# Sixty 16 KB runs of one head of tile 41 stored apart, computed in eight groups ahead of tiles 40 to 47

## The chip, the cores and the metric

The kernel runs on one core of a Trainium2 chip. The metric is the device time of one execution in microseconds (us). The kernel before takes 300.39 us, the median of three runs (300.27 to 300.64). A profiled execution is a separate one: 300.63 us, of which the trace covers a span of 298.8 us from the first to the last instruction.

## The reference

```python
batch, n_heads, seq_t, seq_s, channels = 8, 12, 512, 512, 64
x: (8, 12, 512, 64) float32;  y: (8, 12, 512, 64) float32

def reference(x, y):
    return np.einsum('bhtc,bhsc->bhts', x, y).astype(np.float32)
```

There are 96 heads. For each, a 512 x 64 matrix is multiplied by the transpose of another, and a 512 x 512 float32 result of 1 MB is written. Inputs are 2 x 12.6 MB, the output is 100.7 MB, so four fifths of all traffic are stores.

## The kernel before

**Tiles.** An output tile holds two heads, u = 0 and u = 1, four heads apart in memory. There are 48 of them (o = 0 to 47), four to each of 12 groups. A tile is a slot of SBUF of 128 partitions x 4096 float32, 2 MB. Partition 2q + u holds eight neighbouring output rows of head u, rows 8q to 8q + 7, one after the other: 16 KB that are also contiguous in DRAM. Such 16 KB are called a run here: a tile has 64 runs of each head. There are five slots; loads of x and y (2 MB each, 12 in all) use them too.

**Preparing a group.** ACT, DVE and POOL cast loaded x and y to bf16 into a buffer `keep` (`compress`, the copies at L139 and L141). DVE and POOL spread x so that the two heads of a tile stand in different rows of the contraction with zeros between (`mix`, L141). DVE transposes x and y by 32 x 32 blocks (`transposes`, L206 and L215) into xT and yT, of which there are two each, for even and odd groups. `prepare(i)` emits the transposes of group i and the mixing for group i + 1. From about 62 us on all inputs are loaded, and `keep` falls empty bit by bit.

**A tile.** Eight matmuls of 128 x 128 by 128 x 512 make it, four into each half of PSUM, pm0 and pm1 (`four`, L229 to L237). ACT copies each half into the slot (`result`, L330, the ACTIVATE at L337; 128 x 2048 float32). Then SP issues the 2 MB store (`store`, L323, L328). PE's stream is a loop, `all_products` (L240): six turns of eight tiles, with waits on two semaphores, `ev` for ACT's evictions and `tr` for the transposes.

**Order.** Each engine runs its instructions in the order in which the Python code emits them; `emit` and `need` add the semaphore waits. A slot is free for the tile five later once its store has landed. A DMA is issued by SP in order too: an SP instruction that waits holds up the stores behind it. A store of 128 partitions is spread over 16 DMA engines, eight runs each; each engine works through its own queue in order.

**The corner.** `SPLIT` is tile 41. Of head u = 0 of this tile only a quarter of each run, 4 KB (`N` = 2 x 512 elements, the first two of eight rows), is stored from the slot, by an extra SP store behind that of head u = 1. The other six rows of each run (12 KB, `LEFT` = 6) are computed a second time by `corner` (L257): DVE picks the columns of xT that belong to chosen runs into `picked` (L275), so that the runs land on chosen partitions; PE multiplies them in eight groups of up to four matmuls (96 or 16 rows of PSUM, L295), inside the loop's sixth turn under an `If`; DVE and ACT take turns to copy the groups into the emptied part of `keep` (L141 and L139); and three DMAs store them: by SP 20 runs that lie on 4 partitions ("corner", L314), by POOL 12 runs on 3 partitions and 32 runs on 8 partitions ("side"). `FEW` lists these sets: partitions (in fours) from, to, and runs on each.

In the order of instructions the corner stands between tile 41 and tile 42. On PE the list `held` of its matmuls and waits is put into the loop at that place, and ends with a wait for the last copies of both PSUM halves (L307). On ACT and DVE the copies stand behind the evictions of tile 41, and SP waits for all copies before its corner DMA, which stands ahead of the store of tile 42.

The last lines of the order before:

```python
        for o in range(V, V * NH):
            result(o, slot())
            if o == SPLIT:
                corner()
            if o % V == V - 1:
                prepare(o // V + 2)
        all_products()
        need("pool", [("dmaside", ticks["dmaside"])])
        need("dve", [("dmacorner", ticks["dmacorner"])])
```

V is 4, NH is 12.

Of the kernel before, what the change touches and what calls it, by code (L numbers as in the profile page):

```python
# [9 lines left out]
def kernel(  # L10
# [22 lines left out]
    nc = tc.nc  # L33
# [9 lines left out]
    K = 8  # L43
    E = R // K
    D = 32
    SLOTS = 5
    TURNS = NH // 2
    SPLIT = V * NH - 2 * V + 1
    LEFT = 6
    N = (K - LEFT) * S  # L50
    GROUP = 4
    FEW = ((0, 4, 5), (5, 8, 4), (16, 24, 4))
    fp32 = mybir.dt.float32
    bf16 = mybir.dt.bfloat16
    u32 = mybir.dt.uint32
# [27 lines left out]
    engines = {"act": nc.scalar, "dve": nc.vector, "pool": nc.gpsimd, "pe": nc.tensor, "sp": nc.sync}  # L83
    sems, ticks, known, snaps, writer, readers = {}, {}, {e: {} for e in engines}, {}, {}, {}

    def need(name, points, known_by=None, held=None):

        best = {}
        for p, v in points:
            if known[name].get(p, 0) < v:  # L90
                best[p] = max(best.get(p, 0), v)
        for p, v in list(best.items()):
            if any(snaps[q, w].get(p, 0) >= v for q, w in best.items() if q != p):
                del best[p]
        if known_by is not None:
            assert all(p in dict(known_by) and v <= dict(known_by)[p] for p, v in best.items())
        for p, v in best.items():
            if held is not None:
                held.append((p, v))
            elif known_by is None:  # L100
                engines[name].wait_ge(sems[p], v)  # L101
            known[name][p] = v
            for q, w in snaps[p, v].items():
                known[name][q] = max(known[name].get(q, 0), w)

    lanes = {"act": ("act", "ev"), "dve": ("dve", "tr")}

    def emit(name, make, reads=(), writes=(), dma=None, lane=None, known_by=None, held=None):

        points = [writer[r] for r in (*reads, *writes) if r in writer]  # L110
        points += [v for w in writes for v in readers.get(w, ())]
        if name == "pool" and name in ticks:
            points.append((name, ticks[name]))
        need(name, points, known_by, held)
        p, step = (lane or name, 1) if dma is None else (f"dma{dma}", 16)
        if p not in sems:
            sems[p] = tc.alloc_semaphore(p)
        if held is not None:
            held.append(make)
        elif make is not None:  # L120
            make().then_inc(sems[p], step)
        at = (p, ticks.get(p, 0) + step)
        ticks[p] = at[1]
        snaps[at] = {**known[name], p: at[1]}
        if dma is None:
            for q in lanes.get(name, (name,)):
                snaps[at][q] = ticks.get(q, 0)
        for r in reads:
            readers.setdefault(r, []).append(at)
        for w in writes:  # L130
            writer[w], readers[w] = at, []

    made_slots, loaded, held = [], {}, []
    in_front = ["dve", "pool", "dve", "act"]

    def copy(name, dst, src, reads, writes):
# [12 lines left out]
    def slot():  # L149
        made_slots.append(len(made_slots) % SLOTS)  # L150
        return made_slots[-1]
# [71 lines left out]

    def products(o, k):
        half, pm = o // V % 2, k // 4
        emit("pe", None, [("xT", half), ("yT", half)], [("pm", pm)],
             known_by=[("ev", 2 * o + pm + 1), ("tr", o // V + 1)])

    def four(j, pm):  # L229
        half, h = divmod(j, V)  # L230
# [9 lines left out]
    def all_products():  # L240

        with nc.tensor.Fori(0, TURNS, 1) as t:
            for j in range(2 * V):
                if j % V == 0:
                    nc.tensor.wait_ge(sems["tr"], t * 2 + j // V + 1)
                for pm in range(2):
                    nc.tensor.wait_ge(sems["ev"], t * (4 * V) + 2 * j + pm + 1)
                    four(j, pm).then_inc(sems["pe"], 1)
                if j == SPLIT % (2 * V):
                    with nc.tensor.If(t == SPLIT // (2 * V)):  # L250
                        for step in held:
                            if callable(step):
                                step().then_inc(sems["pe"], 1)
                            else:
                                nc.tensor.wait_ge(sems[step[0]], step[1])

    def corner():  # L257

        half, h = divmod(SPLIT % (2 * V), V)
        xT = xTs[half].bitcast(bf16).rearrange("p (k h q u) -> p k h q u", k=K, h=V, u=2)  # L260
        yT = yTs[half].bitcast(bf16)
        most = max(many for _, _, many in FEW)
        kept = keep[:, :most * LEFT * S].bitcast(fp32)
        runs = kept.rearrange("p (j n) -> p j n", j=most)
        dst = ov[SPLIT // V, h][:, 0, N:]
        picked = keep[:, 3 * NG * R // 2 * D:].bitcast(bf16)[:, :most * LEFT * 96].rearrange(
            "p (j k m) -> p j k m", j=most, k=LEFT
        )
        under = [("yb", 1, b, ch) for b in range(NG - 3, NG - 1) for ch in range(2)]
        first = 0  # L270
        for lo, hi, many in FEW:
            rows = (hi - lo) * many
            emit(
                "dve",
                lambda: nc.vector.tensor_copy(  # L275
                    picked[:, :many, :, 4 * lo:4 * hi:4],
                    xT[:, K - LEFT:, h, first:first + rows, 0].rearrange("p k (e j) -> p j k e", j=many),
                ),
                [("xT", half)],
                [("picked", lo)] + (under if lo == 0 else []),  # L280
            )
            first += rows
        places = [[("xk", i)] for i in range(NG - 1)]
        for i in range(0, NG - 1, 2):
            places.append([("yb", 0, b, ch) for b in (i, i + 1) if b < NG - 1 for ch in range(2)])
        banks = [divmod(b, LEFT) for b in range(most * LEFT)]
        for g in range(0, len(banks), GROUP):
            part = banks[g:g + GROUP]
            pm = g // GROUP % 2
            m = 96 if part[0][0] < most - 1 else 16  # L290

            def make(part=part, pm=pm, m=m):

                for b, (j, k) in enumerate(part):
                    last = nc.tensor.matmul(  # L295
                        pms[pm][:m, b, :], picked[:, j, k, :m], yT[:, h * S:(h + 1) * S],
                        start=True, stop=True,
                    )
                return last

            emit("pe", make, [("picked", lo) for lo, _, _ in FEW] + [("yT", half)], [("pm", pm)], held=held)
            copy(
                "act" if pm else "dve", kept[:m, g * S:(g + len(part)) * S],
                pms[pm].rearrange("p j s -> p (j s)")[:m, :len(part) * S],
                [("pm", pm)], places[g // GROUP],
            )
        need("pe", [v for pm in range(2) for v in readers[("pm", pm)]], held=held)  # L307
        first = 0
        for lo, hi, many in FEW:
            rows = (hi - lo) * many  # L310
            name = "pool" if lo else "sp"
            emit(
                name,
                lambda: engines[name].dma_start(  # L314
                    dst[first:first + rows].rearrange("(e j) n -> e j n", j=many),
                    runs[4 * lo:4 * hi - 3:4, :many],
                ),
                reads=[w for place in places for w in place],
                dma="side" if lo else "corner",
            )  # L320
            first += rows

    def store(o, s):  # L323
        i, h = divmod(o, V)
        to, src = ov[i, h], slots[s]
        parts = [(to, src)] if o != SPLIT else [(to[:, 1], src[1::2]), (to[:, 0, :N], src[0::2, :N])]
        for to, src in parts:
            emit("sp", lambda: nc.sync.dma_start(to, src), reads=both(s), dma=s)  # L328

    def result(o, s):  # L330

        for k in range(0, K, 4):
            pm = k // 4
            products(o, k)
            emit(
                "act",
                lambda: nc.scalar.activation(  # L337
                    slots[s][:, k * S:(k + 4) * S], pms[pm].rearrange("p j s -> p (j s)"), COPY
                ),
                [("pm", pm)],  # L340
                [("slot", s, pm)],
                lane="ev",
            )
        store(o, s)
# [9 lines left out]
    with tc.tile_critical():  # L354
# [36 lines left out]
                transposes(1)  # L391
        prepare(2)
        for o in range(V, V * NH):
            result(o, slot())
            if o == SPLIT:
                corner()
            if o % V == V - 1:
                prepare(o // V + 2)
        all_products()
        need("pool", [("dmaside", ticks["dmaside"])])  # L400
        need("dve", [("dmacorner", ticks["dmacorner"])])
        for i, name in enumerate(("dve", "dve", "dve", "dve", "act")):
# [31 lines left out]
```

## Time and profile before

| | us |
|---|---|
| median of three runs | 300.39 (300.27 to 300.64) |
| the profiled execution | 300.63 |
| its span | 298.8 |
| outside the span | 1.8 |
| ACT busy | 217.9 (73%) |
| DVE busy | 161.6 (54%) |
| PE busy | 144.7 (48%) |
| POOL busy | 57.9 (19%) |
| moved by DMA | 125.87 MB, 421 GB/s over the span |

How to read the profile. The page gives the span in 40 equal slices of 7.47 us, with each engine's busy share in tenths, the clock granted to TensorE (PEclk), the share of time in which the 16 DMA engines were busy, and the rate in GB/s. The groups of instructions give for each line, engine and shape the count, the busy time and the mean of one in ns, and then how long the engine was idle ahead of them and what ended that. The timeline lists instructions in order of time, neighbours of one kind merged: start, time, engine, line and tile, count, and the idle time ahead with what ended it. The stage table gives busy time of each engine in chosen stretches of the span, with the clock, the DMA share and the rate. The trace also holds every DMA packet with its start, its time, its size and its queue, and the moment at which each of the 16 DMA engines reports its part of a transfer.

### The profile page before, as it was taken

What the parts mean: (1) busy time and instruction counts of PE and PEld (TensorE: products, weight loads), DVE (VectorE), ACT (ScalarE), POOL (GpSimd) and SP (SyncE); (2) the same over time, 40 slices, a digit from 0 to 9 for tenths busy, and PEclk for the clock granted to TensorE, in tenths of its full rate; (3) what the DMA queues carried; (4) which work ended last, traced back from release to release, by engine and by line L of the source; (5) the groups of instructions that cost most, each with busy time, mean ns of one, the idle gap of its engine ahead of it and who ended that gap; (6) DMA issues with size and microseconds to landing.
All of it is one profiled execution on the core that took longest, in us unless ns stands there. A gap on an engine that the chain in (4) does not pass through costs nothing.

```text
span 298.8 us, 1363 instructions
## 1 busy us (share of the span) xinstructions
PE 144.7 (48%) x408; PEld 39.3 (13%) x414; DVE 161.6 (54%) x80; ACT 217.9 (73%) x113; POOL 57.9 (19%) x26
## 2 busy tenths in 40 slices
PE   0000040547665663867475665676475667475400
PEld 0000010111111110211111111111111112121100
DVE  2167897999929594915809439076292535600000
ACT  1665676999999996786868686767777775589900
POOL 3399999991000000000000000000000000010000
PEclk9999995657789997565956767756857767979965
DMA  7999999999999999999999999999999999999997
GB/s 265 430 428 432 430 430 428 428 432 432 425 432 430 434 428 429 434 430 428 430 432 429 432 436 428 430 436 423 425 432 434 430 421 428 421 388 430 421 421 316
DMA packets 8875, 125.87 MB, mean 421 GB/s; under 512 B 1128, under 2 KB 1128, under 8 KB 1192
## 3 DMA queue, kind: packets, MB, share of 16 engines
q1 hardware_dynamic: 8680, 125.29, 98.6%
q0 software_dynamic: 192, 0.54, 0.5%
q8 instruction: 1, 0.02, 0.0%
q14 instruction: 2, 0.02, 0.0%
HBM read 25.17 MB, written 100.66 MB: 421 GB/s over the span
## 4 chain that ended last, share of the span: by engine, by line
DMA 54%; ACT 27%; issue 5%; PE 4%; DVE 3%; another core or an unknown queue 1%; SPq 0%; ACTq 0%
DMA out_dram<-slot 41%; ACT slot L337 25%; DMA slot<-in_y_dram 7%; DMA slot<-in_x_dram 6%; DVE keep L141 3%; ACT keep L139 2%; PE pm L295 2%; PE pm L234 2%; SPq L157 0%; ACTq L101 0%; SPq L429 0%; SPq L354 0%
## 5 line engine op out<-in xcount | busy, mean ns | idle before, releaser
L337 ACT ACTIVATE slot<-pm 128x2048 f32<-128x2048 f32 x96 | 173.7, 1894 | 38.2 <-DMA out_dram<-slot 35.0
L234 PE MATMUL pm<-yT,xT 128*128 128x512 bf16 x378 | 135.6, 502 | 132.0 <-ACT slot L337 92.4
L206 DVE STREAM_TRANSPOSE xT<-xb 128x2048 uint32<-128x2048 uint32 x12 | 46.8, 3897 | 69.4 <-PE pm L234 67.0
L234 PEld LDWEIGHTS pm<-yT,xT 128*128 128x128 bf16 x384 | 35.9, 114 | 230.7 <-ACT slot L337 152.0
L139 ACT ACTIVATE keep<-slot 128x4096 bf16<-128x4096 f32 (+1 forms) x12 | 36.5, 3044 | 21.5 <-DMA slot<-in_x_dram 16.3
L141 DVE COPY xb<-keep 32x2048 bf16<-32x2048 bf16 x36 | 47.0, 1305 | 1.0
L141 DVE CAST keep<-slot 64x2048 bf16<-64x2048 f32 x12 | 36.1, 3010 | 17.1 <-DMA slot<-in_y_dram 16.9
L314 POOL DMA_DIRECT2D out_dram<-keep x2 | 1.1, 558 | 192.6 <-DVE keep L141 192.6
L141 POOL COPY xb<-keep 32x2048 bf16<-32x2048 bf16 x12 | 36.2, 3017 | 9.2 <-ACT keep L139 8.4
L215 DVE STREAM_TRANSPOSE yT<-keep 128x1024 uint32<-128x1024 uint32 x12 | 23.1, 1928 | 0.0
L141 POOL CAST keep<-slot 64x2048 bf16<-64x2048 f32 x6 | 17.8, 2973 | 1.4 <-DMA slot<-in_y_dram 0.8
L141 DVE COPY keep<-pm 96x2048 f32<-96x2048 f32 (+1 forms) x4 | 9.1, 2285 | 10.5 <-PE pm L295 10.5
L295 PE MATMUL pm<-yT,keep 128*96 128x512 bf16 (+1 forms) x30 | 9.2, 446 | 4.9 <-DVE keep L141 2.8
L139 ACT ACTIVATE keep<-pm 96x2048 f32<-96x2048 f32 (+1 forms) x4 | 6.6, 1657 | 5.4 <-PE pm L295 5.4
L295 PEld LDWEIGHTS pm<-yT,keep 128*96 128x96 bf16 (+1 forms) x30 | 3.4, 130 | 11.0 <-DVE keep L141 4.5
L371 DVE MEMSET xb<- 128x2048 uint32 x1 | 1.8, 1765 | 1.4 <-SPq L354 1.4
L139 ACT ACT_TABLE_LOAD x1 | 1.3, 1283 | 1.0 <-SPq L354 1.0
L371 POOL MEMSET xb<- 128x2048 uint32 x1 | 1.8, 1823 | 0.0
L362 POOL DMA_DIRECT2D spare<-in_x_dram x1 | 0.7, 701 | 1.2 <-SPq L354 1.2
L275 DVE COPY keep<-xT 128x120 bf16<-128x120 bf16 (+2 forms) x3 | 0.7, 355 | 0.0
L418 POOL MEMSET const-float32-0.0<- 128x1 f32 x1 | 0.1, 98 | 0.2 <-issue 0.2
L418 POOL MEMSET const-float32-1.0<- 128x1 f32 x1 | 0.1, 98 | 0.0
(2 smaller groups left out, 0.2 us busy)
## 6 DMA issues: line engine op xcount, KB each, us to landing
out_dram<-slot SPq DMA_DIRECT2D x47, 2048.0 KB, 20.5
slot<-in_x_dram SPq DMA_DIRECT2D x6, 2048.0 KB, 17.7
slot<-in_y_dram SPq DMA_DIRECT2D x6, 2048.0 KB, 20.8
out_dram<-slot SPq DMA_DIRECT2D x1, 1024.0 KB, 16.9
out_dram<-keep POOLq DMA_DIRECT2D x1, 384.0 KB, 6.1
out_dram<-slot SPq DMA_DIRECT2D x1, 256.0 KB, 18.6
out_dram<-keep SPq DMA_DIRECT2D x1, 240.0 KB
out_dram<-keep POOLq DMA_DIRECT2D x1, 144.0 KB, 5.6
```

Source lines behind the costliest of these rows:

```text
L139: lambda: nc.scalar.activation(dst, src, COPY)
L141: else engines[name].tensor_copy(dst, src),
L206: lambda: nc.vector.transpose(xTs[half].rearrange("p (k r e) -> p k e r", k=K, e=E), xbs[half].rearrange("p (k e c) -> p k e c", k=K, e=E),),
L215: lambda: nc.vector.transpose(yTs[half].rearrange("p (r j) -> p j r", r=D), ybs[half][b].rearrange("p (j c) -> p j c", c=D),),
L234: last = nc.tensor.matmul(pms[pm][:, b, :], xT[:, 4 * pm + b, h, :], yT[:, h * S:(h + 1) * S], start=True, stop=True,)
L275: lambda: nc.vector.tensor_copy(picked[:, :many, :, 4 * lo:4 * hi:4], xT[:, K - LEFT:, h, first:first + rows, 0].rearrange("p k (e j) -> p ...
L295: last = nc.tensor.matmul(pms[pm][:m, b, :], picked[:, j, k, :m], yT[:, h * S:(h + 1) * S], start=True, stop=True,)
L314: lambda: engines[name].dma_start(dst[first:first + rows].rearrange("(e j) n -> e j n", j=many), runs[4 * lo:4 * hi - 3:4, :many],),
L337: lambda: nc.scalar.activation(slots[s][:, k * S:(k + 4) * S], pms[pm].rearrange("p j s -> p (j s)"), COPY),
L362: lambda: nc.gpsimd.dma_start(spare[0:17:4, :, :D // 2], xv[0, 0:5].rearrange("p (a b c) -> p a b c", a=2, c=D)[:, :, 0, :D // 2]),
L371: lambda: engines[name].memset(xbs[half], 0.0),
L418: nc = _bacc.Bacc("TRN2", target_bir_lowering=False, num_devices=1)
```

## The change

The work of the corner is taken apart into three functions and spread.

- The runs stored apart are now 60 whole runs (16 KB, all eight rows) of head u = 0, four runs on each of 15 partitions (`MANY` = 4), instead of 64 runs of 12 KB. The remaining four runs of that head are stored from the slot, by a store of their own of four partitions (`APART` = 60). Bytes in all are the same.
- `pick` (DVE, three copies) is emitted after tile 36.
- `piece(g, pm)` is one group of four matmuls with 96 rows and its copy by DVE, and is emitted one ahead of each tile from 40 to 47, eight groups in all. A group uses one half of PSUM; the tile behind it begins with the other half: for even tiles the order of halves is pm1, pm0. So the halves strictly take turns on PE. ACT no longer copies any of these groups.
- `send` issues the three DMAs after the eighth group, ahead of the evictions and the store of tile 47: SP 16 runs on 4 partitions, POOL 12 runs on 3 and 32 runs on 8.
- PE's loop has five turns (40 tiles, `LOOPED`) and no `If`; tiles 40 to 47 and the groups follow it as straight code.

```diff
-    TURNS = NH // 2
-    SPLIT = V * NH - 2 * V + 1
-    LEFT = 6
-    N = (K - LEFT) * S
+    TURNS = NH // 2 - 1
+    LOOPED = 2 * V * TURNS
+    SPLIT = LOOPED + 1
+    MANY = 4
     GROUP = 4
-    FEW = ((0, 4, 5), (5, 8, 4), (16, 24, 4))
+    GROUPS = MANY * K // GROUP
+    FEW = ((0, 4), (5, 8), (16, 24))
+    APART = MANY * sum(hi - lo for lo, hi in FEW)
...
     def products(o, k):
         half, pm = o // V % 2, k // 4
-        emit("pe", None, [("xT", half), ("yT", half)], [("pm", pm)],
-             known_by=[("ev", 2 * o + pm + 1), ("tr", o // V + 1)])
+        reads, writes = [("xT", half), ("yT", half)], [("pm", pm)]
+        if o < LOOPED:
+            emit("pe", None, reads, writes, known_by=[("ev", 2 * o + pm + 1), ("tr", o // V + 1)])
+        else:
+            emit("pe", lambda: four(o % (2 * V), pm), reads, writes)
...
-                if j == SPLIT % (2 * V):
-                    with nc.tensor.If(t == SPLIT // (2 * V)):
-                        for step in held:
-                            if callable(step):
-                                step().then_inc(sems["pe"], 1)
-                            else:
-                                nc.tensor.wait_ge(sems[step[0]], step[1])
-
-    def corner():
+
+    def pick():
...
-                    picked[:, :many, :, 4 * lo:4 * hi:4],
-                    xT[:, K - LEFT:, h, first:first + rows, 0].rearrange("p k (e j) -> p j k e", j=many),
+                    picked[:, :, :, 4 * lo:4 * hi:4],
+                    xT[:, :, h, first:first + rows, 0].rearrange("p k (j e) -> p j k e", j=MANY),
...
+    def piece(g, pm):
+
+        half, h = divmod(SPLIT % (2 * V), V)
+        yT = yTs[half].bitcast(bf16)
+
+        def make():
+
+            for b in range(GROUP):
+                j, k = divmod(g * GROUP + b, K)
+                last = nc.tensor.matmul(
+                    pms[pm][:96, b, :], picked[:, j, k, :], yT[:, h * S:(h + 1) * S],
+                    start=True, stop=True,
+                )
+            return last
+
+        emit("pe", make, [("picked", lo) for lo, _ in FEW] + [("yT", half)], [("pm", pm)])
+        copy(
+            "dve", kept[:96, g * GROUP * S:(g + 1) * GROUP * S],
+            pms[pm].rearrange("p j s -> p (j s)")[:96],
+            [("pm", pm)], places[g],
+        )
+
+    def send():
+
+        dst = ov[SPLIT // V, SPLIT % V][:, 0]
         first = 0
-        for lo, hi, many in FEW:
-            rows = (hi - lo) * many
+        for lo, hi in FEW:
+            rows = (hi - lo) * MANY
             name = "pool" if lo else "sp"
             emit(
                 name,
                 lambda: engines[name].dma_start(
-                    dst[first:first + rows].rearrange("(e j) n -> e j n", j=many),
-                    runs[4 * lo:4 * hi - 3:4, :many],
+                    dst[first:first + rows].rearrange("(j e) n -> e j n", j=MANY),
+                    runs[4 * lo:4 * hi - 3:4],
                 ),
...
-        parts = [(to, src)] if o != SPLIT else [(to[:, 1], src[1::2]), (to[:, 0, :N], src[0::2, :N])]
+        parts = [(to, src)] if o != SPLIT else [(to[:, 1], src[1::2]), (to[APART:, 0], src[2 * APART::2])]
...
     def result(o, s):
 
-        for k in range(0, K, 4):
+        for k in (4, 0) if o >= LOOPED and o % 2 == 0 else (0, 4):
             pm = k // 4
...
         for o in range(V, V * NH):
+            if o == LOOPED:
+                all_products()
+            if o >= LOOPED:
+                piece(o - LOOPED, o % 2)
+            if o == V * NH - 1:
+                send()
             result(o, slot())
-            if o == SPLIT:
-                corner()
             if o % V == V - 1:
                 prepare(o // V + 2)
-        all_products()
+            if o == LOOPED - V:
+                pick()
         need("pool", [("dmaside", ticks["dmaside"])])
```

More of the change, by code (lines that the diff above doesn't have):

```diff
@@ L84, with need @@
     sems, ticks, known, snaps, writer, readers = {}, {}, {e: {} for e in engines}, {}, {}, {}
-    def need(name, points, known_by=None, held=None):
+    def need(name, points, known_by=None):
         best = {}
@@ L97, in need @@
         for p, v in best.items():
-            if held is not None:
-                held.append((p, v))
-            elif known_by is None:
+            if known_by is None:
                 engines[name].wait_ge(sems[p], v)
@@ L106, with emit @@
     lanes = {"act": ("act", "ev"), "dve": ("dve", "tr")}
-    def emit(name, make, reads=(), writes=(), dma=None, lane=None, known_by=None, held=None):
+    def emit(name, make, reads=(), writes=(), dma=None, lane=None, known_by=None):
         points = [writer[r] for r in (*reads, *writes) if r in writer]
@@ L113, in emit @@
             points.append((name, ticks[name]))
-        need(name, points, known_by, held)
+        need(name, points, known_by)
         p, step = (lane or name, 1) if dma is None else (f"dma{dma}", 16)
@@ L117, in emit @@
             sems[p] = tc.alloc_semaphore(p)
-        if held is not None:
-            held.append(make)
-        elif make is not None:
+        if make is not None:
             make().then_inc(sems[p], step)
@@ L131, in emit @@
             writer[w], readers[w] = at, []
-    made_slots, loaded, held = [], {}, []
+    made_slots, loaded = [], {}
     in_front = ["dve", "pool", "dve", "act"]
@@ L248, in all_products @@
                     four(j, pm).then_inc(sems["pe"], 1)
-                if j == SPLIT % (2 * V):
-                    with nc.tensor.If(t == SPLIT // (2 * V)):
-                        for step in held:
-                            if callable(step):
-                                step().then_inc(sems["pe"], 1)
-                            else:
-                                nc.tensor.wait_ge(sems[step[0]], step[1])
-    def corner():
+    kept = keep[:, :MANY * K * S].bitcast(fp32)
+    runs = kept.rearrange("p (j n) -> p j n", j=MANY)
+    picked = keep[:, 3 * NG * R // 2 * D:].bitcast(bf16)[:, :MANY * K * 96].rearrange(
+        "p (j k m) -> p j k m", j=MANY, k=K
+    )
+    places = [[("xk", i)] for i in range(NG - 1)]
+    for i in range(0, NG - 1, 2):
+        places.append([("yb", 0, b, ch) for b in (i, i + 1) if b < NG - 1 for ch in range(2)])
+    places[-1] += [("yb", 1, 0, ch) for ch in range(2)]
+    def pick():
         half, h = divmod(SPLIT % (2 * V), V)
         xT = xTs[half].bitcast(bf16).rearrange("p (k h q u) -> p k h q u", k=K, h=V, u=2)
[L261 to L268, printed above, removed]
         under = [("yb", 1, b, ch) for b in range(NG - 3, NG - 1) for ch in range(2)]
         first = 0
-        for lo, hi, many in FEW:
-            rows = (hi - lo) * many
+        for lo, hi in FEW:
+            rows = (hi - lo) * MANY
             emit(
@@ L282, in corner @@
             first += rows
[L283 to L307, printed above, removed]
+    def piece(g, pm):
[14 more added lines that the diff above has]
+            [("pm", pm)], places[g],
+        )
+    def send():
+        dst = ov[SPLIT // V, SPLIT % V][:, 0]
         first = 0
-        for lo, hi, many in FEW:
-            rows = (hi - lo) * many
+        for lo, hi in FEW:
+            rows = (hi - lo) * MANY
             name = "pool" if lo else "sp"
```

## The prediction, made before the changed kernel ran

> **What bounds the kernel now.** I read first the slices of the page, for the resource that is never idle.
>
> ```profile
> PEclk9999995657789997565956767756857767979965
> DMA  7999999999999999999999999999999999999997
> GB/s 265 430 428 432 430 430 428 428 432 432 425 432 430 434 428 429 434 430 428 430 432 429 432 436 428 430 436 423 425 432 434 430 421 428 421 388 430 421 421 316
> ```
>
> DMA is full between the ends, at about 430 GB/s, with one dip: slice 35, 261 to 269 us, 388 GB/s. Second, the stage table around that dip.
>
> ```profile
> 261.00:266.00 5.00, 4.12 (x11) 1.29 (x12) 0.04 (x1) 3.29 (x2) 1.11 (x2) 0.66 0.97 401
> 266.00:268.00 2.00, 1.11 (x5) 0.31 (x4) 0.00 (x0) 2.00 (x3) 0.00 (x0) 1.00 0.67 275
> 268.00:297.00 29.00, 8.29 (x32) 2.47 (x32) 0.00 (x0) 16.06 (x10) 0.00 (x0) 0.81 1.00 425
> ```
>
> From 266 to 268 us the engines are busy for 67%. Counted in the packets, all 16 have work without a gap from 5 us to 266.5 us and again from 267.7 us to the end of the data at 297.28 us; the hole costs 0.80 us per engine in the mean. Third, the timeline, for who makes the hole.
>
> ```profile
> 247.59 2.29 DVE L141 COPY keep<-pm 96x2048 f32<-96x2048 f32 x1 [6.16 <-PE pm L295]
> 248.16 1.91 SPq L328 DMA_DIRECT2D out_dram<-slot  x2
> 249.99 1.87 ACT L139 ACTIVATE keep<-pm 96x2048 f32<-96x2048 f32 x1 [1.85 <-PE pm L295]
> ...
> 261.07 0.82 SPq L314 DMA_DIRECT2D out_dram<-keep  x1
> 261.35 1.11 POOL L314 DMA_DIRECT2D out_dram<-keep  x2 [192.64 <-DVE keep L141]
> ...
> 262.71 21.35 ACT L337 ACTIVATE slot<-pm 128x2048 f32<-128x2048 f32 x12 [2.51 <-remote]
> ...
> 266.38 18.24 SPq L328 DMA_DIRECT2D out_dram<-slot  x6
> ```
>
> Tile 41's stores go out at 248.16, the next full store at 266.38: ACT evicts no tile from 248.1 to 262.7 us while the corner passes through PSUM. Until then stores had followed every 4.9 us. Eighteen us without a store empty a queue that is about 19 us deep (a store takes 20.5 us from issue to landing).
>
> **How the 16 engines stand.** This decides what the hole is worth. I followed each engine's packets through tile 41. Ten come dry at 266.5 to 266.9 us. Four, those of the SP corner (five 12 KB packets each), at 267.01, 267.08, 267.32 and 267.40. One has no 12 KB packet and is dry at 266.78: it is the slow one, which had been 2.2 us behind. One ends at 267.64, just when tile 42's first packets start on all engines (267.63 to 267.78). I call it the late engine. So the hole costs most engines 1.1 us and the late one nothing; it puts all in step, and the last packets end at 297.12 to 297.28 us. The end is set by the last engine, hence removing the hole is worth 0.80 us only if no engine stays behind.
>
> **The change part by part.**
>
> *The hole.* ACT drops 6.6 us of corner copies, PE's groups stand singly between tiles, DVE makes eight copies of 2.29 us instead of four. Does the feed then keep up? PE finishes tile 39 at 235.2 and DVE starts the last transposes there (3.88 + 1.90 us, to 240.9), so the first group's copy ends near 243.3. Half pm0 of tile 40 waits for that, is multiplied (1.04 us for four matmuls at full clock) and evicted (1.87), so tile 40's store leaves near 247.0 instead of 243.2. From there a tile takes two evictions and a group, 1.04 + 2.29 us in the other half, about 5.0 us with the waits. At half clock four matmuls take 1.89 us and three groups with their gaps about 6.0. Tile 46's store then leaves between 277 and 283.6, its first packets 1.25 us later (266.38 to 267.63 in the hole), and the ten engines need it at 261.6 + 36 x 0.614 = 283.7. So the feed is hidden by a lead of 5.4 us at full clock, and short by 1.1 us at half. The clock between 230 and 262 was 6 to 9 tenths with eight matmuls per tile; with twelve I expect it nearer the top, a lead of some 3 us.
>
> *The engines' shares.* The sets keep their first sizes (4, 3 and 8 partitions), so I take it that they fall on the same engines. From tile 41 on an ordinary engine has 4 packets of head 1, 48 of tiles 42 to 47 and 4 of the apart runs: 56 packets of 16 KB. The four SP engines also get the 4-row remainder, one each: 57. The slow one has 52. A packet costs 0.608 us on an engine out of step with the others (the late one: 4.86 us per tile of eight over the last 16 tiles) and 0.614 in the pack (4.91 us per tile). Starts of tile 41 are the ends above less the packets followed:
>
> - ten engines: about 261.6 + 56 x 0.614 = 296.0 (the one at 266.9: 296.4);
> - the latest SP engine: 261.99 + 57 x 0.608 to 0.614 = 296.65 to 296.99;
> - the late engine: 262.72 + 56 x 0.608 to 0.614 = 296.77 to 297.10;
> - the slow one: 263.70 + 52 x 0.617 = 295.8.
>
> I take 296.85, nearer the out-of-step price because both engines have been out of step so far. Against 297.28 that is 0.43 us less. The relief of the slow engine (64 KB for 48 KB, 0.61 us) buys nothing, since it was not last.
>
> *Moves on the queues.* SP's waits: the corner DMA (0.82 us of issue) now stands between the stores of 46 and 47 and waits for the eighth DVE copy, which PE makes ahead of tile 47; store 47 waits longer for ACT anyway. The 64-piece store of 4 KB (1.37 us of issue) becomes one of four rows. POOL's two DMAs (1.11 us) come at about 278 instead of 261; they landed in 6 us, so near 284, well ahead of the end. The three picks (0.73 us) move into DVE's idle 9.36 us before the last transposes; the piece copies stand behind those. No POOL or ACT work waits for them. At nothing, covered by the stores in the queue; uncovered, the picks would cost 0.7 us.
>
> *PE's code.* The loop loses a turn and the `If`, and about 230 instructions of straight code follow. The trace shows two loads of code on DMA queues other than the stores' at 115.5 us (16 KB and 8 KB) and one at 161.4 us (8 KB). Each delayed one DMA engine: the 16 KB one by 1.31 us (two neighbouring packets took 0.99 and 0.94 us), the 8 KB ones by 0.67. The 16 KB one starts 6 ns after PE's branch back, and it is what made the late engine late. Whether PE's longer code brings another is not to be seen here: bounds 0 and +1.31 us, on some one engine. I take 0, because the sixth turn's straight `If` block of some 70 instructions brought none. [...]
>
> *The sum.* Profiled execution 300.63 = 298.84 span + 1.80 outside. The data end 0.43 earlier, and the 1.56 us behind them are unchanged: 300.20. The median is 0.24 below the profiled execution: 299.96.
>
> **Rivals.**
>
> *No engine stays late.* Should the code load at 115.5 us move or fall on the slow engine, or the pack run at 0.608, the SP engines set the end: 261.66 to 261.99 + 57 x 0.608 = 296.3 to 296.65, gain 0.63 to 0.96, 299.4 to 299.8. For it: packets after the hole, in step, cost 0.617, and staggered ones less. Against: the early program is the same, so the lateness should recur.
>
> *Slower: another code load.* PE runs into its straight code at about 235 us, and a 16 KB load lands on the same queue and the late engine: 296.85 + 1.31 = 298.16, so 301.27. It decides from a delay of 0.43 + 0.60 = 1.03 us on that engine; on one of the ten it would end at 297.3, no change; an 8 KB load on the late engine gives 300.63. For it: PE's code grows by more than half. Against: once in 298 us so far.
>
> *The hole only moves.* If PE stays at half clock, every one of the last tiles takes 6 us, the ten engines come dry for 1.1 us near 284, all are in step behind it as now, and about 0.2 us of the gain is left with tile 47 late as well: 300.2 to 300.6. For it: PEclk of 5 in eight of the 40 slices. Against: denser work has gone with a higher clock here (9 tenths or more from 269 to 284).
>
> **How the numbers follow.** The forecast (299.7 to 300.2) has 0.48, no late engine 0.17, another code load 0.17, the moved hole or a small load 0.13; 0.05 are unnamed. 0.2% is 0.60 us, about what a measurement here can tell from no change: faster means below 299.79, slower above 300.99. Faster: 0.15 of the second case and 0.10 of the forecast's edge, 0.25. Slower: 0.17 and 0.02 of the rest, 0.19. Within: 0.56. The range takes 299.5 to 301.3: without the code load 0.22 would be left out, so it is in.
>
> **What would show it.** Right: no slice below 420 GB/s between 261 and 290; stores 40 to 47 issued about 5 us apart from 247 on; eight DVE copies of 96x2048 near 2.29 us; the last store's 16 reports spread by 0.8 us or more (0.23 before) with the late engine last. Wrong: a code load on a DMA queue between 200 and 290 us, DMA dry near 284, or a spread below 0.4 with an end below 296.6.

## The result and the profile after

The changed kernel takes 301.50 us (median of seven runs, 301.42 to 301.59) against 300.39 us (300.27 to 300.72, seven runs): a ratio of 1.0033, 95% interval 1.0023 to 1.0043. It is slower, where 299.96 was forecast, and 0.2 us outside the range. The profiled execution has 301.5 us and a span of 299.7.

The slices of the changed kernel, as of the page before:

```profile
span 299.7 us, 1336 instructions
...
PEclk9999999998799997595677596677756579999755
DMA  7999999999999999999999999999999999999995
GB/s 271 426 433 433 426 424 431 431 429 429 435 429 429 437 429 428 435 429 429 435 431 425 435 431 424 437 433 424 426 440 424 426 422 418 442 396 422 426 424 245
```

The dip of slice 35 is still there, 396 GB/s where it was 388, though the DMA row shows nothing idle. The last slice carries 245 GB/s where it carried 316. The stage table says what kind of dip it is (columns as before; the last two are DMA share and GB/s):

```profile
262.00:264.00 2.00, 1.36 (x7) 0.43 (x6) 1.31 (x1) 1.23 (x1) 0.00 (x0) 1.00 1.16 451
264.00:266.00 2.00, 1.47 (x6) 0.41 (x4) 0.20 (x1) 2.00 (x2) 0.00 (x0) 1.00 0.95 336
...
290.00:296.00 6.00, 0.00 (x0) 0.00 (x0) 0.00 (x0) 0.00 (x0) 0.00 (x0) 0.50 0.96 410
296.00:299.50 3.50, 0.00 (x0) 0.00 (x0) 0.00 (x0) 0.00 (x0) 0.00 (x0) 0.50 0.18 75
```

From 264 to 266 us the engines are busy and move 336 GB/s. (1.16 and 0.95 belong together, and so do 451 and 336: a packet counts where it starts, and long ones cross the edge of the stages. Over 262 to 268 us it is 393 GB/s at a share of 1.01, a line that is shown with the first experiment.) That is no hole: packets run, and run slowly. At the end, from 296 us on, few engines still work.

The feed is as it was forecast. The clock of the stage in which it starts, and the timeline from the fourth group on (ahead of tile 43; PE's weight loads left out):

```profile
240.00:262.00 22.00, 13.11 (x46) 4.46 (x47) 11.13 (x6) 14.80 (x8) 0.00 (x0) 0.92 1.01 427
```

```profile
255.15 1.06 PE L289 MATMUL pm<-yT,keep 128*96 128x512 bf16 x4 [0.86 <-ACT slot L334]
256.25 2.29 DVE L139 COPY keep<-pm 96x2048 f32<-96x2048 f32 x1 [2.84 <-PE pm L289]
256.92 1.04 PE L235 MATMUL pm<-yT,xT 128*128 128x512 bf16 x4 [0.71 <-ACT slot L334]
258.00 3.65 ACT L334 ACTIVATE slot<-pm 128x2048 f32<-128x2048 f32 x2 [1.13 <-PE pm L235]
...
277.67 0.71 SPq L311 DMA_DIRECT2D out_dram<-keep  x1
277.95 1.12 POOL L311 DMA_DIRECT2D out_dram<-keep  x2 [209.32 <-DVE keep L139]
280.76 0.55 SPq L325 DMA_DIRECT2D out_dram<-slot  x1
```

Group, copy by DVE, tile, two evictions by ACT: 4.8 us per tile, at a clock of 1.00 from 262 to 268 us. The single SP issues in the trace stand at 246.99 (tile 40), 252.12, 256.89, 261.67, 266.44, 271.22 and 275.99 (tile 46). All 16 engines have packets without a gap until 295 us.

The answer lies in the packets. Followed engine by engine, nine engines write their last data at 295.7 to 296.1 us, and seven at 297.29, 297.40, 297.50, 297.54, 297.71, 298.15 and 298.23. The reports of the last store on the 16 engines spread over 2.37 us (0.23 before). Packets of 16 KB normally take 611 ns (the median). Those over 700 ns after 240 us are few:

```
changed kernel, packets over 700 ns (start us, ns; 16 KB stores unless noted)
246.84  854   247.70  945   248.64  929 (16 KB load of code)   249.55 1006
263.43  727   263.73  847   263.92 1900   263.98 2059   264.18 1271
264.24 2315   264.30 2182   264.59 1293   265.46 1053   265.91  871
```

There are two groups. At 247 to 251 us one engine carries a load of code: in the kernel before, that load came at 115.52 us. At 263.4 to 266.8 us six engines are slow, four with one packet of 1.9 to 2.3 us each and two with a row of packets of 0.7 to 1.3 us. This is the moment at which the four-row store of tile 41, issued at 252.66, reaches the front: the 20 reports of tile 41's two stores come between 264.26 and 266.90 us.

### The profile page after: what moved, and what is told of

The parts are those of the page before. It is cut to its first block, busy times and chain, and to the rows that moved or that the text cites. A ratio compares the mean times of both kernels' runs of the same rounds, so it can differ in the third digit from the quotient of the medians.

```text
span 299.7 us, 1336 instructions
## 1 busy us (share of the span) xinstructions
PE 142.4 (48%) x409; PEld 39.1 (13%) x416; DVE 170.6 (57%) x84; ACT 211.9 (71%) x109; POOL 57.9 (19%) x26
## 4 chain that ended last, share of the span: by engine, by line
DMA 48%; ACT 30%; PE 5%; DVE 5%; issue 5%; SPq 0%; ACTq 0%; DVEq 0%
DMA out_dram<-slot 35%; ACT slot L334 27%; DMA slot<-in_y_dram 7%; DMA slot<-in_x_dram 6%; PE pm L235 5%; DVE keep L139 3%; ACT keep L137 2%; DVE xT L204 1%; DVE yT L213 1%; PE pm L289 1%; SPq L155 0%; ACTq L101 0%; SPq L431 0%; DVEq L101 0%; SPq L351 0%
## 5 line engine op out<-in xcount | busy, mean ns | idle before, releaser
L235 PE MATMUL pm<-yT,xT 128*128 128x512 bf16 x377 | 132.7, 491 | 133.0 <-ACT slot L334 87.7
L235 PEld LDWEIGHTS pm<-yT,xT 128*128 128x128 bf16 x384 | 35.2, 112 | 229.8 <-ACT slot L334 144.1
L139 DVE COPY keep<-pm 96x2048 f32<-96x2048 f32 x8 | 18.3, 2282 | 18.3 <-PE pm L289 18.3
L289 PE MATMUL pm<-yT,keep 128*96 128x512 bf16 x32 | 10.2, 450 | 3.4 <-ACT slot L334 3.4
L289 PEld LDWEIGHTS pm<-yT,keep 128*96 128x96 bf16 x32 | 3.9, 140 | 9.4 <-ACT slot L334 4.6
L271 DVE COPY keep<-xT 128x128 bf16<-128x128 bf16 (+2 forms) x3 | 0.8, 370 | 0.0
```

The source lines that it names most:

```text
L139: else engines[name].tensor_copy(dst, src),
L235: last = nc.tensor.matmul(pms[pm][:, b, :], xT[:, 4 * pm + b, h, :], yT[:, h * S:(h + 1) * S], start=True, stop=True,)
L271: lambda: nc.vector.tensor_copy(picked[:, :, :, 4 * lo:4 * hi:4], xT[:, :, h, first:first + rows, 0].rearrange("p k (j e) -> p j k e", j=M ...
L289: last = nc.tensor.matmul(pms[pm][:96, b, :], picked[:, j, k, :], yT[:, h * S:(h + 1) * S], start=True, stop=True,)
```

## The experiments

Every ratio is to the kernel before on the same chip. Theory A is an assumption: the four rows (q = 60 to 63) lie on partitions 120, 122, 124 and 126, which the last two engines read in every full store; the first four engines, which carry the four-row store (they are called the SP engines here), read there too, and six engines share what otherwise serves two. This makes the SP engines last; the next would be the engine of the moved code load. The packets in the trace bear no engine's number, and no trace shows which engine reads which partitions, so the theory is put to the test by moving the rows. An engine's own partitions are below those that theory A gives it.

### The four rows on the engines' own partitions; the code load early; both; the spreading alone

The first edit chooses other rows for the slot store, with three regular sets for the rest:

```diff
+    ROWS = (slice(1, 32, 2), slice(8, 32, 2), slice(32, 64))
...
-                    dst[first:first + rows].rearrange("(j e) n -> e j n", j=MANY),
+                    dst[rows].rearrange("(j e) n -> e j n", j=MANY),
...
-        parts = ... [(to[:, 1], src[1::2]), (to[APART:, 0], src[2 * APART::2])]
+        parts = ... [(to[:, 1], src[1::2]), (to[0:8:2, 0], src[0:16:4])]
```

> The changed kernel, but the four runs stored from the slot are q = 0, 2, 4, 6 (partitions 0, 4, 8, 12, one in each of the first four engines' share of a store) instead of q = 60 to 63 (partitions 120 to 126, the share of the last two engines). Bytes, packets per engine and instructions are the same. Theory A (four engines read partitions that the last two also read, and six engines share two ways into SBUF): the packets of 0.85 to 2.3 us between 263 and 266 us are gone, the four SP engines end near 296.9, and the engine of the 16 KB code load, 1.97 us late at tile 40, ends last at 261.6 + 1.97 + 56 x 0.608 = 297.6; against 298.25 now that is 0.65 us less, 300.85. Rival B (a store of four rows is dear wherever its rows lie): long packets stay, 301.5. Rival C (the code load alone sets the end): long packets may go, the time stays within 0.15 of 301.5.

Measured: 300.82 us, ratio 1.0009 (1.0000 to 1.0018). No store packet between 262 and 268 us is long, and the stage that moved 393 GB/s in the changed kernel moves 429. The two lines, of the changed kernel and then of this one:

```profile
262.00:268.00 6.00, 3.87 (x16) 1.15 (x14) 3.51 (x2) 4.10 (x3) 0.00 (x0) 1.00 1.01 393
```

```profile
262.00:268.00 6.00, 4.06 (x16) 1.34 (x16) 3.51 (x2) 3.89 (x3) 0.00 (x0) 1.00 1.01 429
```

One engine ends last at 297.59, the next at 297.20. The sum gave 297.6 for the code load's engine, and the last one carries packets of POOL's sets, so it is none of the SP engines. A store of four rows is not dear in itself (rival B falls). But the median is still 0.35 us over the kernel before's on that chip (300.47), with an interval that only just begins at 1.0000.

The second edit puts an `If` that is never taken into PE's loop, so that its code is about as long as before:

```diff
                     four(j, pm).then_inc(sems["pe"], 1)
+                if j == SPLIT % (2 * V):
+                    with nc.tensor.If(t == TURNS):
+                        for pm in (0, 1, 0, 1, 0, 1, 0, 1):
+                            four(j, pm)
```

> The changed kernel with an If that is never taken, with 32 matmuls in it, in PE's loop behind tile 1 of each turn: about as much code as the If block of the kernel before had. It is meant to bring the 16 KB code load back from 248.6 us to about 115 us. Theory A (the four-row store sets the end): the load moves, its engine is 1.2 us late at tile 40 instead of 1.97, and the time stays near 301.4, because the four SP engines still end at 298.2. Rival C (the code load sets the end): 296.8 instead of 298.25, 300.1 to 300.7. If the load does not move, 301.5 by both.

Measured: 301.53 us, ratio 1.0034 (1.0021 to 1.0046). The 16 KB load moves to 115.24 us. The time does not move: the long packets near 264 are there (eight, of 1.2 to 2.2 us), and the last engines still end at 298.22 and 298.26. The code load alone does not set the end (rival C falls).

Both edits:

> Both edits together. Theory A, with the forecast's own sum as it stands without the two causes: SP engines 296.65 to 297.0, the late engine 296.8 to 297.1, so 300.0 to 300.2. Rival C: the same as with the early code alone. Rival B: 301.4. If the sum itself was wrong (another engine is last), it stays above 300.5 with no long packets and an early load.

Measured: 300.26 us, ratio 0.9991 (0.9982 to 1.0000). Repeated on two other chips, in answer to

> The version with both edits again, to stand on the same chip as the two others: 300.26 as before, 0.4 above the version in which POOL stores the four rows.

and

> The version with both edits, again on the same chip as the one with eight runs: 300.27, 0.3 above it by theory A.

it took 300.29 both times (0.9994, interval 0.9985 to 1.0003, and 0.9992, 0.9984 to 1.0001). In the first of these profiles the last engines end at 297.04 and 297.07. So early code, which bought nothing beside the long packets, buys 0.56 us without them. Different engines were late for two different reasons, and the later ones hid the other. The time alone, 300.26 to 300.29 against 300.46 to 300.50 for the kernel before, is not clear of no change: the three intervals end at 1.0000, 1.0003 and 1.0001.

The spreading alone keeps the kernel before's 64 runs of 12 KB and its 4 KB store:

```diff
-    FEW = ((0, 4), (5, 8), (16, 24))
+    FEW = ((0, 4, 5), (5, 8, 4), (16, 24, 4))
...
+        part = [divmod(b, LEFT) for b in range(g * GROUP, min((g + 1) * GROUP, MOST * LEFT))]
+        m = 96 if part[0][0] < MOST - 1 else 16
...
-        (to[APART:, 0], src[2 * APART::2])
+        (to[:, 0, :N], src[0::2, :N])
```

> One part of the change alone: the groups spread over tiles 40 to 47 and the straight code, but with the 64 runs of 12 KB, 5 on each of the first 4 partitions, and the 4 KB store of 64 rows of the kernel before. No four-row store. Theory A: no long packets near 264, the code load near 248 and its engine last, 263.5 + 56 packets' worth, 297.6: 300.8 to 300.9. Rival D (the spreading itself costs, by the feed or by the packets): 301.4 or more. By the forecast without the code load it would be 300.1.

Measured: 300.76 us, ratio 1.0007 (0.9998 to 1.0016). The load of code is at 248.01 us and one engine ends alone at 297.41, the next at 296.83. Rival D, with 301.4 or more, falls. With the `If` added:

> The spread groups with the 12 KB runs of the kernel before, and the early code load. Neither cause is left, so this is what closing the hole is worth alone. By the forecast's sum: SP engines 261.99 + 4 x 0.61 + 0.64 + 2.33 + 48 x 0.61 = 296.7 to 297.0, the late engine 296.8: 300.0 to 300.2, 0.3 to 0.45 below the kernel before. Rival D (closing the hole buys nothing, since some engine always stays late): 300.4 to 300.5.

Measured: 300.21 us, ratio 0.9989 (0.9980 to 0.9998). No long packets, no late code load, the last data at 296.77. This is what closing the hole is worth by itself: 0.26 us in the medians of that chip (300.47), with an interval from 0.06 to 0.60 us. It is the lowest median here, by 0.05 us, and that much can't be told from the version with both edits. Its end, in the stage table:

```profile
262.00:268.00 6.00, 3.92 (x16) 1.34 (x16) 3.51 (x2) 4.04 (x3) 0.00 (x0) 1.00 1.02 431
290.00:296.00 6.00, 0.00 (x0) 0.00 (x0) 0.00 (x0) 0.00 (x0) 0.00 (x0) 0.50 0.97 414
296.00:298.00 2.00, 0.00 (x0) 0.00 (x0) 0.00 (x0) 0.00 (x0) 0.00 (x0) 0.50 0.06 25
```

431 GB/s where the hole was, and behind 296 us 25 GB/s over 2.0 us, where the changed kernel has 75 over 3.5.

### The dose

The four rows on partitions that, by theory A, one ordinary engine each reads (q = 32, 36, 40, 44), with early code:

```diff
-        (to[APART:, 0], src[2 * APART::2])
+        (to[REST:REST + 16:4, 0], src[2 * REST:2 * REST + 32:8])   # REST = 32
...
```

> The changed kernel with the early code load (If never taken in the loop) and the four runs of the slot store at q = 32, 36, 40, 44: partitions 64, 72, 80, 88, each in the share of another ordinary engine, none in that of the four SP engines. Theory A (engines that read the same partitions' way share its rate): each of the four packets takes about 2 x 0.61 = 1.2 us instead of 2 to 2.3, its partner engine loses 0.6 us, the SP engines end near 297.07 + 0.6 = 297.7, and the time lies between the own-port and the far version: 300.26 + 0.6 = 300.85. Rival B2 (any read outside an engine's own partitions is slow by itself, whoever else reads there): packets of 2 us as before and 301.5. Rival B3 (only partitions 120 to 126 are slow): no long packets, 300.26.

Measured: 300.49 us, ratio 0.9999 (0.9990 to 1.0008). Nine packets take over 700 ns, all between 263.4 and 265.8 us: seven of 1.02 to 1.22 us, about twice 0.61, and two of 0.71 and 0.75. By theory A that is what four pairs of engines give, where one packet meets two of its partner's. In the changed kernel, where it counts three readers, it was 1.90 to 2.32. None takes 2 us here, so B2 falls as it was put; and long packets come without partitions 120 to 126, so B3 falls too. The rows also go to other places in DRAM; but this version and the one with own partitions both store four separate rows, the one with long packets and the other without, so that alone is not it. The stage lies between the changed kernel's 393 GB/s and 429:

```profile
262.00:268.00 6.00, 3.73 (x16) 1.25 (x16) 3.00 (x2) 4.70 (x3) 0.00 (x0) 1.00 1.02 412
```

The dose is right, but the time is 0.36 us below what I expected: three engines end at 297.14 and 297.15, not at 297.7. The reports of the stores show where it went, in part. Leaving out the slow engine, the latest is 1.50 us behind the first at tile 42, against 1.00 in the version with both edits, so the long packets cost 0.50 of the 0.6 us expected; at the last store it is 1.22 behind, against 1.06. Some 0.3 us were made up on the way. Why is open.

### Two attempts at a better version

The SP engines were last with 57 packets. In the first attempt POOL stores the four rows (q = 32, 34, 36, 38), in the place in its turn where I thought it would use the engines that read these partitions (that its transfers take the engines in turn was my assumption, which no trace shows). POOL's other sets are rearranged for it, with tiny transfers to fill its turn.

> The changed kernel with the early code load, and the four runs left in the slot (q = 32, 34, 36, 38) stored by POOL, in the turn that puts them on four ordinary engines which read these partitions anyway. The SP engines then have 56 packets instead of 57 (end 297.07 - 0.61 = 296.45), four ordinary ones 57 (296.05 + 0.61 = 296.66), the late one 296.65: 0.4 us below the version with both edits, 299.85, and 0.6 below the kernel before. If the end is set by something else than the last engine's packets, the time stays at 300.26. If POOL's turns fall on other engines than I think, packets of 1.2 us or more appear again and it is 300.8 or more.

Measured: 303.93 us, ratio 1.0114 (1.0098 to 1.0129). The rate falls where POOL's transfers run; the stage table of this version:

```profile
256.00:260.00 4.00, 2.46 (x10) 0.62 (x8) 2.29 (x1) 2.87 (x3) 0.00 (x0) 1.00 0.99 389
282.00:290.00 8.00, 0.00 (x0) 0.00 (x0) 0.00 (x0) 0.00 (x0) 0.00 (x0) 0.53 1.00 344
```

All engines busy, 344 GB/s, with packets of 1.0 to 1.36 us from 283 to 297 us. By theory A the sets fell on engines that do not read their partitions otherwise, and much of the apart store paid the price of two readers; the trace does not show the engines. I thought the turn was carried over between executions, since this version used 28 places and the kernel before 16.

> The version in which POOL stores the four rows, once more, with one more tiny POOL transfer of four partitions at the end, into a buffer that nobody reads. Theory E: POOL's transfers go to the 16 engines in turn, as many engines as partitions, and the turn carries over from one execution to the next; the kernel before takes 5 + 3 + 8 = 16 of them and so begins anew each time, the version at 303.93 took 28 and stood elsewhere in each execution, now it takes 32. Then no packet near 257 us or after 283 us takes 1.0 to 1.3 us, the SP engines have 56 packets and end near 296.5, and the time is 299.85. Rival: the turn is not what misplaced them; two-way packets stay, 303 to 304.

Measured: 303.96 us, ratio 1.0116 (1.0101 to 1.0132), with the same packets of 1.1 to 1.2 us at 257. Theory E falls. The same without the `If`:

> The same without the If, so with the code load at 248 us: its engine ends last, at 297.55: 300.8 by theory A, as with the own ports; if no long packets are left, the difference to the version with the If is the price of the late code load alone, 0.5 to 0.9 us.

303.84 us, 1.0113 (1.0098 to 1.0129), where 300.8 was expected: the code load is at 247.42 us again, and nothing can be told from it, because the long packets set the end. Why POOL's transfers had long packets here stays open.

The last attempt leaves eight runs to SP, on the first eight engines and, by theory A, their own partitions, with three apart runs on the corner's:

```diff
+    FEW = ((0, 4, 3), (5, 8, 4), (16, 24, 4))
+    ROWS = (slice(16, 40, 2), slice(40, 64, 2), slice(1, 64, 2))
...
+        (to[0:16:2, 0], src[0:32:4])
```

> The changed kernel with the early code load and eight runs left in the slot (q = 0, 2, ..., 14), stored by SP from partitions 0, 4, ..., 28: one on each of the first eight engines, from partitions that they read anyway. 56 runs are stored apart, three on each of the SP corner's four partitions, four on the others. Packets from tile 41 on: 56 on the SP engines and on most others, 57 on the three next to the slow one, 53 on the slow one. Theory A: no long packets, the SP engines end near 297.05 - 0.61 = 296.45, the last is the late engine or one of 57, 296.65 to 296.8: 299.9 to 300.05, 0.3 below the version with both edits and 0.4 to 0.5 below the kernel before. If long packets of about 1.2 us appear between 262 and 266 us, an engine reads another's partitions and it is 300.5 or more.

Measured: 300.26 us, ratio 0.9995 (0.9986 to 1.0004), no faster than the version with both edits on the same chip (300.29), where 0.3 us less was expected. No packet of 1.2 us appears, so by theory A the placing was right. One engine ends alone at 297.09, the next at 296.84. The last one carries four packets of POOL's sets, so it is none of the SP engines: they were relieved, and another took their place. Three engines have 57 packets; if one of them is also delayed by a code load, it ends there, but that was not established.

## Why the prediction was wrong, step by step

- *What bounds the kernel, and the hole.* Right. The engines are never dry between 5 and 295 us. Tile 40's store left at 246.99 (forecast 247.0) and tile 46's at 275.99 (277 at full clock), at a clock of 0.92 between 240 and 262. The rival that the hole only moves did not occur.
- *The last engine sets the end; the hole is not worth 0.80.* Right, and more so than I said. Nine engines end at 295.7 to 296.1, where 296.0 was summed for the ten, and this bought nothing. In all fourteen profiled executions, from 300.04 to 303.83 us, the time is 3.26 to 3.35 us more than the moment at which the last engine's data end.
- *"The four SP engines also get the 4-row remainder, one each: 57."* This step failed. I priced each of these packets at 0.608 to 0.614 us like any other. They took 1.90, 2.06, 2.18 and 2.32 us, and two more engines lost 1.2 us each (three packets of 3.05 and 3.01 us in all, for 1.83). I looked at the engines on which the store falls, and not at the partitions it reads. By theory A the corner's partitions 0, 4, 8, 12 give each of its engines a row of its own share; 120 to 126 belong to two others. Six engines on what serves two make three packets of 0.61 us for each, 1.8 us: an estimate of mine from the price of a packet and theory A's count of readers. That six engines share "two ways into SBUF", as the first expectation has it, no run shows. The traces agree with the count in order: 1.90 to 2.32 us where it has three readers, somewhat more than the estimate, 1.02 to 1.22 where it has two, none long where it has one. Taking this out is worth 0.68 us (301.50 to 300.82) with the late load and 1.27 us (301.53 to 300.26, on one chip) without.
- *"I take 0, because the sixth turn's straight `If` block of some 70 instructions brought none."* This failed too, in a way that I had no case for. No further 16 KB load came; the one at 115.5 us came at 248.64 instead, in the stretch that I had named as the sign of a wrong forecast (200 to 290 us). Its engine is 1.97 us late at tile 40 instead of 1.21. Later is worse in two ways: there are fewer tiles in which the pack loses its lead (in the kernel before the engine's lateness fell from 1.55 us at 227 us to 1.21 at 262), and the load cost 1.90 us (four packets of 854, 945, 929 and 1006 ns for three stores) where it cost 1.31 before. Moving it back is worth 0.56 us once the long packets are gone (300.82 to 300.26), and nothing beside them (301.50 and 301.53).
- *"The early program is the same, so the lateness should recur."* Wrong for the same reason: the loop's code was shorter by the `If`, and the load moved with it (248.64 us without, 115.24 us with an `If` put back).
- *The shares without the two causes: "I take 296.85, nearer the out-of-step price".* The count was right, the price was not. In the version with both edits the latest SP engines end at 297.04 and 297.07, forecast 296.65 to 296.99. From the forecast's start that is 0.615 us for each of 57 packets, even above the price in the pack. Though they end 1 us behind the pack, the last 14 packets of the two took 616 and 617 ns in the mean, and those of the pack 615 to 617; in the changed kernel the last 14 of the two latest, 2.1 us behind, took 611. So the reading of 0.617 behind the hole as the price of being in step does not hold: the mean of all 16 KB packets from 268 us on is 617 ns in the version with both edits too, against 612 between 115 and 190 us. What raises it is open. In time 300.26 to 300.29 against 299.96.
- *The sign.* The rival of another code load gave 301.27, with a chance of 0.17, from a mechanism close to the smaller part of the cause. That it comes within 0.23 us of the measured time is luck: with a late load and the four rows moved it was 300.82. Of the miss of 1.54 us, 0.68 are the place of the four rows and 0.56 the load, in the order in which they were taken out, and 0.30 are left with both out, of which the later end of the SP engines is 0.2. (The 0.68 compares two occasions, on which the kernel before took 300.39 and 300.47.)

## What to carry to other kernels

When the 16 DMA engines are the bound, the end is the end of the slowest of them (here the time was 3.26 to 3.35 us more than the end of its data, in all fourteen profiled executions), so an edit is priced engine by engine, in packets, and not by mean rate or bytes. By theory A a small store of a few partitions should be read by the engines that serve these partitions in the full store; here the packets took 1.02 to 1.22 us instead of 0.61 where it has two engines meet and 1.90 to 2.32 where it has three, and two other engines lost 1.2 us each. A slow stage with all engines busy (393 GB/s at a share of 1.01) was the sign of this; an idle share (275 GB/s at 0.67 in the kernel before) was the sign of a feed that failed. When such a cause is taken out and nothing is gained, another engine may be late just behind: only both edits together showed what each was worth.

## What the runs showed of the hardware

- Packets of 16 KB took 0.61 us (the median) where theory A has one reader of a group of partitions, 1.02 to 1.22 where it has two (rows at q = 32, 36, 40, 44), and for the extra readers 1.90 to 2.32 where it has three (q = 60 to 63, the changed kernel). The number of readers is an assumption that the moved rows bear out; the trace does not name the engines.
- A 16 KB load on the queue marked "instruction" (PE's code, I take it: in the kernel before it starts 6 ns after PE's branch back) delayed one DMA engine by 1.3 to 1.4 us at 115 us, and by 1.89 to 1.90 us at 247 to 249 us in four versions, where the two store packets ahead of it were slow as well (766 to 854 and 945 to 1018 ns). Why was not tried.
- That load moved with an `If` block in PE's loop: it came at 114.7 to 115.5 us, at the loop's second branch back, with the block in it, taken later or never, and at 247.4 to 248.6 us, in the straight code, without. What triggers it is open.
- A packet took 617 ns in the mean from 268 us on, against 612 between 115 and 190 us, in the kernel before, whose engines stood in step, and in the version with both edits, whose engines did not. The cause is open.
